# Opening of a hybrid decoder layer: half of the squares and of the modulation rows moved to VectorE, copies and factor work reordered

## The chip, the cores and the metric

The kernel runs on one core of one Trainium2 chip. The metric is the device time of one execution in microseconds (us); shorter is better. A core has TensorE (PE, matmuls), VectorE (DVE), ScalarE (ACT), GpSimd (POOL) and SyncE (SP, which issues most DMAs). Each engine works through its own queue of instructions in order and waits on semaphores for results of the others.

## What is computed

One layer, float32, for 1024 tokens of 2048 features:

```python
mod = silu(c) @ w_ada + b_ada              # c: (1, 2048), w_ada: (2048, 6144)
shift, scale, gate = split(mod, 3)
h = rms_norm(x, gain) * (1 + scale) + shift   # x: (1024, 2048)
proj = h @ w_in                            # (1024, 8192): q, k, v, z of two groups of 8 heads
oa = stick_breaking_attention(...) * silu(z_sb)
ob = group_norm(retention(...)) * silu(z_r)
out = x + gate * (concat(oa, ob) @ w_out)
```

The change lies in what comes ahead of `proj` and in its first part: the row norms of x, `mod`, h and its first products.

## The kernel before, in words

**Products in three passes.** A float32 product is made of three fast ones (`mm3`, L184 to L187): each operand is cut into a high part, which ScalarE writes (L172 for weights, L595 for h), and a low part, which VectorE writes as a difference (L174, L597). `wp` holds four high and four low tiles of weights, so that a block's weights can be cut two blocks ahead and no more.

**The opening.** 16 blocks of 128 features (`kc`) are walked in the order `KCS`, by the index p. Tokens come in two halves of 512 (hf 0 and 1).

1. `load_x` brings x of tokens 0 to 511 as 16 tiles of 128 tokens by 512 features. `x_squares` (L510) lets ScalarE square each tile and sum its rows; `x_scale` (L519) works out 1/rms with 13 small VectorE instructions on a column and scales the tiles, half on VectorE, half on ScalarE.
2. w_ada is read in chunks `cc` of 256 columns, 2 MB each (`load_ada`): chunks 0 to 7 give the scale, chunks 8 to 15 the shift. `ada_sums` (L559) adds up a chunk's 16 rows of each partition with 16 products on PE (each is two passes of the array, 32 instructions of 32x256 in all), into a bank `accp` that VectorE copies out (L569). `ada_mod` (L576) adds over the partitions with two small products `mod`, and VectorE turns them into `mods` (L585, L586) or `shift` (L588).
3. `x_turn` (L538) turns four 128x128 pieces of x on PE into a bank, and copies the bank to `xT`, by VectorE for odd p of the first half (L550), else by ScalarE (L552). `make_h` (L590) writes h's two parts from `xT` and `mods`.
4. `start_mm` multiplies h of block p by 7 heads of weights ("first": z of the retention group), 21 matmuls to a block. In the first half's loop over p, sums of chunk p//2+2 come at the start of each odd block, and `ada_mod` of the chunk after p's within each even block, behind head 4.

**The second half** (tokens 512 to 1023) does the same with the 16 blocks again. In block p, in PE's order: head 0; `x_turn` of block p+2; heads 1 to 3; then `ada_mod` (even p, whose result is `shift`) or `ada_sums` (odd p); heads 4 to 6. `x_turn`, `ada_sums` and `ada_mod` share one bank, "C", so each waits until the last one's result has been read. `cut_w` cuts the weights of block p+2 at the end of block p, and `add_bias` (L769) multiplies the raw weights by the shift on VectorE.

**Factors.** The rest of `proj` is done as a Strassen-like product, which wants sums and differences of quarters of h. `factors(ks)` (L622) queues them for two k at a time: eight ScalarE instructions `whole` (L629: scale and shift of `xT`; they read `shift`) and B21's parts go to the deque `urgent`, 28 more (differences on VectorE, L635 and L642; high parts on ScalarE, L605; low parts on VectorE, L612, with stores for T2, T1 and B22) go to `background`. Behind each head of the second half, `some` takes one or two from each deque. `factors` is called at the end of blocks 3, 7, 11 and 15; what is left after block 15 runs in the first groups of the next stage.

**The next stage** begins with products `pj` into four banks in which the heads 3 to 6 of "first" have been gathered; ScalarE must have copied them out first (`spill`, zt, L775), behind the cuts of the stage's first weights.

**Order.** PE's order is the order of the program text (`manual_schedule`). On VectorE and ScalarE a scheduler orders the first half's instructions by its own estimates; from the second half on every engine takes the order of the text.

**The end.** `finish_out` (L1475) multiplies the output's last bank by the gate, adds x, and stores 128x512 through SP.

Of the kernel before, what the change touches and what calls it, by code (L numbers as in the profile page):

```python
# [98 lines left out]
def layer_kernel(ctx, tc, x, c, w_ada, b_ada, norm_gain, w_in, sb_q_gain, sb_k_gain, ret_norm_gain, w_out,  # L99
# [410 lines left out]
    def x_squares(ts):  # L510
        ss = sm.tile([P, 2, 4], F32, tag="ss", name=f"ss_{ts[0]}")
        for i, t in enumerate(ts):
            for qt in range(4):
                junk = get(f"junk_{t}_{qt}")
                nc.scalar.activation(junk, xt[t, qt], AF.Square, accum_out=ss[:, i, qt:qt + 1])
                put(junk)
        return ss

    def x_scale(ts, ss):  # L519

        n = len(ts)
        nc.vector.tensor_tensor(ss[:, 0:n, 0:2], ss[:, 0:n, 0:2], ss[:, 0:n, 2:4], op=ALU.add)
        m = sm.tile([P, 2], F32, tag="m", name=f"m_{ts[0]}")
        nc.vector.tensor_tensor(m[:, 0:n], ss[:, 0:n, 0], ss[:, 0:n, 1], op=ALU.add)
        nc.vector.tensor_scalar(m[:, 0:n], m[:, 0:n], 1.0 / D, EPS, op0=ALU.mult, op1=ALU.add)
        y = sm.tile([P, 2], F32, tag="y", name=f"y_{ts[0]}")
        u = sm.tile([P, 2], F32, tag="u", name=f"u_{ts[0]}")
        rsqrt_newton(y[:, 0:n], m[:, 0:n], u[:, 0:n])
        for qt in (0, 2, 1, 3):
            for i, t in enumerate(ts):  # L530
                if i % 2:
                    nc.scalar.activation(xt[t, qt], xt[t, qt], AF.Copy, scale=y[:, i:i + 1])
                else:
                    nc.vector.tensor_scalar(xt[t, qt], xt[t, qt], y[:, i:i + 1], None, op0=ALU.mult)
# [3 lines left out]
    def x_turn(p, g, tag, bufs):  # L538

        kc = KCS[p]  # L540
        xT[kc, g] = get(f"xT{kc}_{g}")
        tp = ps.tile([P, HALF], F32, tag=tag, bufs=bufs, name=f"xtp_{kc}_{g}")
        for t in range(4):
            src = xt[4 * g + t, kc // 4]
            nc.tensor.transpose(tp[:, t * P:(t + 1) * P], src[:, (kc % 4) * P:(kc % 4 + 1) * P], ident)
        left_in[kc // 4, g] -= 1
        if left_in[kc // 4, g] == 0:
            put(*[xt.pop((4 * g + t, kc // 4)) for t in range(4)])
        if p % 2 and g == 0:
            nc.vector.tensor_copy(xT[kc, g], tp)  # L550
        else:
            nc.scalar.activation(xT[kc, g], tp, AF.Copy)  # L552
# [6 lines left out]
    def ada_sums(cc):  # L559
# [3 lines left out]
        for j in range(16):  # L563
            g = j % 4
            nc.tensor.matmul(ap_[32 * g:32 * g + 32, :], silu_z[:, j, :],  # L565
                             ada[cc, j // 2][:, (j % 2) * 256:(j % 2) * 256 + 256], start=j < 4, stop=j >= 12)
        put(*[ada.pop((cc, g)) for g in range(8)])
        acc = get(f"acc_{cc}")
        nc.vector.tensor_copy(acc[:, 0:256], ap_)  # L569
# [129 lines left out]
    sums = {0: ada_sums(0)}  # L699
    for p in range(4):  # L700
        x_turn(p, 0, "pj", 4)
# [3 lines left out]
    for p in range(2):  # L705
        make_h(p, 0)
    for p in range(4, 8):
# [3 lines left out]
    sums[1] = ada_sums(1)  # L711
# [13 lines left out]
    sums[2] = ada_sums(2)  # L725
# [3 lines left out]
    for p in range(2, KC):  # L729
# [7 lines left out]
        if p % 2 and p < KC - 1:  # L737
            sums[cc + 1] = ada_sums(cc + 1)
# [43 lines left out]
    for p in range(KC):  # L782
# [11 lines left out]
        for i, h in enumerate((0, 1, 2, 3, 4, 5, 6) if p < KC - 1 else (3, 4, 5, 6, 0, 1, 2)):  # L794
# [3 lines left out]
            if i == 3 and p % 2 == 0:  # L798
                ada_mod(cc, sums.pop(cc))
            if i == 3 and p % 2 and cc < 15:  # L800
# [3 lines left out]
            if len(urgent) <= 6:  # L804
                some(background, 1 if urgent or i % 4 == 3 else 2)
            some(urgent, 1 if p < KC - 1 else 2)
# [4 lines left out]
        if p % 4 == 3:  # L811
            factors((KCS[p - 3], KCS[p - 2]))
# [662 lines left out]
    def finish_out(n, t, bank_):  # L1475
        x_, y_ = xrs.pop((n, t)), anywhere(f"yt_{n}_{t}")
        nc.vector.tensor_tensor(y_, bank_, gates[n], op=ALU.mult)
# [108 lines left out]
```

## Time and profile before

| | us |
|---|---|
| median of 3 runs | 1971.6 (1971.21 to 1973.71) |
| the profiled execution's own time | 1972.75 |
| its span, first to last instruction | 1971.0 |
| PE busy | 1918.2 (97% of the span) |
| VectorE busy | 1222.5 (62%) |
| ScalarE busy | 800.0 (41%) |
| granted PE clock, mean | 0.995 |

The profiled execution's own time is 1.75 us above its span. A row of a timeline gives the start, the duration, the engine, the source line, the operation and its tiles; in brackets stand the idle time of the engine just before and what ended it. A row of a wait table gives who waited for whom, the sum, the number and the longest. A row of a windows table gives, for each engine, the busy time in that stretch and the number of instructions, then the granted PE clock, the share of the DMA engines and GB/s.

### The profile page before, as it was taken

How to read it: one execution, taken by the hardware profiler on the slowest of the kernel's cores; microseconds unless marked ns; L12 is line 12 of the kernel's file. 1: busy time of each engine (PE TensorE's matmuls, PEld its weight loads, DVE VectorE, ACT ScalarE, POOL GpSimd, SP SyncE). 2: the span in 40 equal slices, each digit the busy share in tenths (PEclk: the TensorE clock that was granted, in tenths of full speed). 3: DMA queues.
4: the chain of work that ended last, by engine and by line, in shares of the span. 5: the costliest groups of instructions: out<-in, count | busy, mean ns of one | idle time of the engine just before them, and what ended most of it. 6: DMA issues, size and time to landing. Idle time of an engine off the chain costs nothing.

```text
span 1971.0 us, 28290 instructions
## 1 busy us (share of the span) xinstructions
PE 1918.2 (97%) x9703; PEld 1573.3 (80%) x9703; DVE 1222.5 (62%) x2389; ACT 800.0 (41%) x1497; POOL 81.1 (4%) x278
## 2 busy tenths in 40 slices
PE   5999899999999999999999999999999999999998
PEld 4776678787888878888888888887888888788887
DVE  4637875346768676867686767865677557634222
ACT  5446663224544454445444544343343554211110
POOL 0000000000110011001100010000000000000000
PEclk9999989999999999999999999999999999999999
DMA  9967797897797679867976798889979738546141
GB/s 321 355 216 262 254 335 268 287 339 261 243 305 262 239 238 302 272 234 241 305 269 240 244 299 270 258 270 295 317 236 284 229 107 282 194 123 198 38 138 64
DMA packets 381724, 487.50 MB, mean 247 GB/s; under 512 B 30734, under 2 KB 201864, under 8 KB 381580
## 3 DMA queue, kind: packets, MB, share of 16 engines
q1 hardware_dynamic: 381192, 485.65, 75.3%
q8 instruction: 76, 1.25, 0.3%
q14 instruction: 68, 0.56, 0.1%
q10 hardware_dynamic: 388, 0.04, 0.0%
HBM read 410.04 MB, written 75.54 MB: 246 GB/s over the span
## 4 chain that ended last, share of the span: by engine, by line
PE 85%; DVE 6%; DMA 5%; ACT 2%; issue 1%; SPq 0%; DVEq 0%; ACTq 0%
PE pj L185 17%; PE pj L187 17%; PE pj L186 16%; PE y L185 5%; PE y L187 5%; PE y L186 5%; PE first L185 2%; PE first L186 2%; PE first L187 2%; PE accp L565 2%; DVE wl L174 1%; PE tp_B L1070 1%; PE zp L185 1%; PE zp L187 1%; PE zp L186 1%
## 5 line engine op out<-in xcount | busy, mean ns | idle before, releaser
L174 DVE TENSOR_TENSOR wl<-A,wh 128x512 fp32r<-128x512 f32 x392 | 272.6, 696 | 315.1 <-ACT wh L172 295.4
L172 ACT ACTIVATE wh<-A 128x512 fp32r<-128x512 f32 x392 | 246.4, 629 | 359.0 <-PE pj L186 340.6
L185 PE MATMUL y<-wh_o,ch 128*128 128x512 f32 x512 | 200.1, 391 | 2.4 <-ACT ch L1412 2.3
L187 PE MATMUL y<-wh_o,cl 128*128 128x512 f32 x512 | 199.6, 390 | 0.0
L186 PE MATMUL y<-wl_o,ch 128*128 128x512 f32 x512 | 199.3, 389 | 0.0
L174 DVE TENSOR_TENSOR wl_o<-wo,wh_o 128x512 fp32r<-128x512 f32 x80 | 54.9, 691 | 173.9 <-ACT wh_o L172 169.9
L172 ACT ACTIVATE wh_o<-wo 128x512 fp32r<-128x512 f32 x80 | 50.4, 630 | 238.4 <-PE y L187 214.2
L388 ACT ACTIVATE c<-pj 128x512 f32<-128x512 f32 x112 | 66.5, 597 | 173.3 <-PE pj L187 148.1
L391 DVE TENSOR_TENSOR c<-pj,c 128x512 f32<-128x512 f32 x112 | 75.0, 688 | 79.2 <-PE pj L187 79.2
L185 PEld LDWEIGHTS y<-wh_o,ch 128*128 128x128 f32 x512 | 96.1, 188 | 24.4 <-ACT ch L1412 3.1
L187 PEld LDWEIGHTS y<-wh_o,cl 128*128 128x128 f32 x512 | 96.1, 188 | 21.1 <-DVE cl L1413 1.1
L186 PEld LDWEIGHTS y<-wl_o,ch 128*128 128x128 f32 x512 | 96.1, 188 | 19.9
L295 DVE TENSOR_TENSOR A<-A,A 128x512 f32<-128x512 f32 x160 | 109.4, 691 | 2.1
L185 PE MATMUL pj<-B21h,wh 128*128 128x512 f32 x232 | 94.5, 407 | 4.4 <-ACT zt L775 4.4
L1050 DVE TENSOR_TENSOR_SCAN om<-om 128x128 f32<-128x128 f32 (+2 forms) x96 | 93.6, 974 | 1.1
L185 PE MATMUL first<-h_hi,wh_first 128*128 128x512 f32 x224 | 92.6, 413 | 1.1 <-ACT h_hi L595 1.1
L187 PE MATMUL pj<-B21h,wl 128*128 128x512 f32 x232 | 92.7, 399 | 0.7 <-DVE wl L174 0.7
L185 PE MATMUL pj<-T1h,wh 128*128 128x512 f32 x232 | 92.5, 399 | 0.0
L185 PE MATMUL pj<-B22h,wh 128*128 128x512 f32 x232 | 92.3, 398 | 0.0
L186 PE MATMUL pj<-B21l,wh 128*128 128x512 f32 x232 | 92.1, 397 | 0.0
L185 PE MATMUL pj<-B11h,wh 128*128 128x512 f32 x232 | 91.7, 395 | 0.0
L187 PE MATMUL pj<-T1h,wl 128*128 128x512 f32 x232 | 90.7, 391 | 0.0
(237 smaller groups left out, 4580.5 us busy)
## 6 DMA issues: line engine op xcount, KB each, us to landing
A<-in_w_in_dram SPq DMA_DIRECT2D x228, 256.0 KB
ada<-in_w_ada_dram SPq DMA_DIRECT2D x128, 256.0 KB
wo<-in_w_out_dram SPq DMA_DIRECT2D x80, 256.0 KB
gr<-in_w_ada_dram SPq DMA_DIRECT2D x64, 256.0 KB
T2h<-fac_T SPq DMA_DIRECT2D x56, 256.0 KB
T2l<-fac_T SPq DMA_DIRECT2D x56, 256.0 KB
T1h<-fac_T SPq DMA_DIRECT2D x56, 256.0 KB
T1l<-fac_T SPq DMA_DIRECT2D x56, 256.0 KB
```

What stands on the lines that cost most here:

```text
L172: nc.scalar.activation(hi[:, 0:n], src[:, 0:n], AF.Copy)
L174: nc.vector.tensor_tensor(lo[:, 0:n], src[:, 0:n], hi[:, 0:n].bitcast(F32), op=ALU.subtract)
L185: nc.tensor.matmul(o, a_hi, b_hi, start=first, stop=False, skip_group_check=on)
L186: nc.tensor.matmul(o, a_hi, b_lo, start=False, stop=False, skip_group_check=on)
L187: nc.tensor.matmul(o, a_lo, b_hi, start=False, stop=last, skip_group_check=on)
L295: nc.vector.tensor_tensor(r[o], r[a], r[b], op=ALU.add if n == 1 else ALU.subtract)
L388: nc.scalar.activation(t, o, AF.Copy)
L391: nc.vector.tensor_tensor(dst[q, cc], o, dst[q, cc], op=ALU.add)
L565: nc.tensor.matmul(ap_[32 * g:32 * g + 32, :], silu_z[:, j, :], ada[cc, j // 2][:, (j % 2) * 256:(j % 2) * 256 + 256], start=j < 4, stop=j ...
L1050: nc.vector.tensor_tensor_scan(rev, rev, rev, init, op0=ALU.mult, op1=ALU.bypass)
L1070: nc.tensor.transpose(banks_[j // 2][:, c0:c0 + P], be[:, j * P:(j + 1) * P], ident)
```

## The change

- `x_squares`: ScalarE squares two of a token tile's four quarters; for the other two VectorE takes `bn_stats`, and `bn_aggr` over both gives mean and variance. `x_scale` puts the two together (two small VectorE instructions more per call, and `bn_aggr`).
- `ada_sums` has a parameter: for chunks 1 to 7 PE sums 8 of the 16 rows, and VectorE adds the other 8, one `scalar_tensor_tensor` of 128x256 each, the first of them from the bank. The copy of the bank falls away there.
- Opening: the turns of blocks 0 and 1 stand ahead of chunk 0's last four products; the copies of blocks 2 and 3 come, in the program text, behind `make_h` of blocks 0 and 1.
- Second half: `ada_mod` and `ada_sums` come behind head 4 in place of head 3. `factors` is called behind `ada_mod` in blocks 2, 6, 10 and 14 (for the same two k), in place of the end of blocks 3, 7, 11 and 15. `some` takes 2 from `background` behind even heads and 1 behind odd ones (or 1 while `urgent` holds something), and 1 from `urgent` in the last block too.
- The last output tile is finished and stored in two halves, by SP and by ScalarE's DMA queue.

```diff
@@ -508,21 +508,28 @@
                               ada_rows[:, 2 * g:2 * g + 2, col:col + 2 * P])
 
     def x_squares(ts):
-        ss = sm.tile([P, 2, 4], F32, tag="ss", name=f"ss_{ts[0]}")
+
+        ss = sm.tile([P, 2, 2], F32, tag="ss", name=f"ss_{ts[0]}")
+        mv = sm.tile([P, 2, 2], F32, tag="xmv", name=f"xmv_{ts[0]}")
         for i, t in enumerate(ts):
-            for qt in range(4):
-                junk = get(f"junk_{t}_{qt}")
-                nc.scalar.activation(junk, xt[t, qt], AF.Square, accum_out=ss[:, i, qt:qt + 1])
+            st6 = sm.tile([P, 2, 6], F32, tag="xst6", name=f"xst6_{t}")
+            for j in range(2):
+                junk = get(f"junk_{t}_{j}")
+                nc.scalar.activation(junk, xt[t, j], AF.Square, accum_out=ss[:, i, j:j + 1])
                 put(junk)
-        return ss
-
-    def x_scale(ts, ss):
-
-        n = len(ts)
-        nc.vector.tensor_tensor(ss[:, 0:n, 0:2], ss[:, 0:n, 0:2], ss[:, 0:n, 2:4], op=ALU.add)
+                nc.vector.bn_stats(st6[:, j, :], xt[t, 2 + j])
+            nc.vector.bn_aggr(mv[:, i, :], st6)
+        return ss, mv
+
+    def x_scale(ts, sums):
+
+        n, (ss, mv) = len(ts), sums
         m = sm.tile([P, 2], F32, tag="m", name=f"m_{ts[0]}")
         nc.vector.tensor_tensor(m[:, 0:n], ss[:, 0:n, 0], ss[:, 0:n, 1], op=ALU.add)
         nc.vector.tensor_scalar(m[:, 0:n], m[:, 0:n], 1.0 / D, EPS, op0=ALU.mult, op1=ALU.add)
+        nc.vector.tensor_tensor(mv[:, 0:n, 0], mv[:, 0:n, 0], mv[:, 0:n, 0], op=ALU.mult)
+        nc.vector.tensor_tensor(mv[:, 0:n, 0], mv[:, 0:n, 0], mv[:, 0:n, 1], op=ALU.add)
+        nc.vector.scalar_tensor_tensor(m[:, 0:n], mv[:, 0:n, 0], 0.5, m[:, 0:n], op0=ALU.mult, op1=ALU.add)
         y = sm.tile([P, 2], F32, tag="y", name=f"y_{ts[0]}")
         u = sm.tile([P, 2], F32, tag="u", name=f"u_{ts[0]}")
         rsqrt_newton(y[:, 0:n], m[:, 0:n], u[:, 0:n])
@@ -535,7 +542,7 @@
 
     left_in = {(qt, g): 4 for qt in range(4) for g in range(2)}
 
-    def x_turn(p, g, tag, bufs):
+    def x_turn(p, g, tag, bufs, now=True):
 
         kc = KCS[p]
         xT[kc, g] = get(f"xT{kc}_{g}")
@@ -546,27 +553,42 @@
         left_in[kc // 4, g] -= 1
         if left_in[kc // 4, g] == 0:
             put(*[xt.pop((4 * g + t, kc // 4)) for t in range(4)])
-        if p % 2 and g == 0:
-            nc.vector.tensor_copy(xT[kc, g], tp)
-        else:
-            nc.scalar.activation(xT[kc, g], tp, AF.Copy)
+
+        def copy():
+            if p % 2 and g == 0:
+                nc.vector.tensor_copy(xT[kc, g], tp)
+            else:
+                nc.scalar.activation(xT[kc, g], tp, AF.Copy)
+        if now:
+            copy()
+        return copy
 
     silu_t = get("silu_z")
     silu_z = silu_t.rearrange("p (j n) -> p j n", n=32)
     nc.vector.memset(silu_t, 0.0)
     nc.vector.tensor_copy(silu_z[:, :, 0], silu_c)
 
-    def ada_sums(cc):
+    def ada_sums(cc, n_pe=16, between=None):
+
 
 
         ap_ = ps.tile([P, 256], F32, tag="C", name=f"accp_{cc}")
-        for j in range(16):
+
+        def row(j):
+            return ada[cc, j // 2][:, (j % 2) * 256:(j % 2) * 256 + 256]
+
+        for j in range(n_pe):
+            if between and j == n_pe - 4:
+                between()
             g = j % 4
-            nc.tensor.matmul(ap_[32 * g:32 * g + 32, :], silu_z[:, j, :],
-                             ada[cc, j // 2][:, (j % 2) * 256:(j % 2) * 256 + 256], start=j < 4, stop=j >= 12)
+            nc.tensor.matmul(ap_[32 * g:32 * g + 32, :], silu_z[:, j, :], row(j), start=j < 4, stop=j >= n_pe - 4)
+        acc = get(f"acc_{cc}")
+        if n_pe == 16:
+            nc.vector.tensor_copy(acc[:, 0:256], ap_)
+        for j in range(n_pe, 16):
+            nc.vector.scalar_tensor_tensor(acc[:, 0:256], row(j), silu_c[:, j:j + 1],
+                                           ap_ if j == n_pe else acc[:, 0:256], op0=ALU.mult, op1=ALU.add)
         put(*[ada.pop((cc, g)) for g in range(8)])
-        acc = get(f"acc_{cc}")
-        nc.vector.tensor_copy(acc[:, 0:256], ap_)
         return acc
 
     mods = cons.tile([P, KC], F32, name="mods")
@@ -696,19 +718,20 @@
     ss = [x_squares((0, 1)), x_squares((2, 3))]
     x_scale((0, 1), ss[0])
     x_scale((2, 3), ss[1])
-    sums = {0: ada_sums(0)}
-    for p in range(4):
-        x_turn(p, 0, "pj", 4)
+    sums = {0: ada_sums(0, between=lambda: [x_turn(p, 0, "pj", 4) for p in range(2)])}
+    copies = [x_turn(p, 0, "pj", 4, False) for p in range(2, 4)]
     ws[0] = start_w(0, 0)
     load_ada(1)
     ada_mod(0, sums.pop(0))
     for p in range(2):
         make_h(p, 0)
+    for copy in copies:
+        copy()
     for p in range(4, 8):
         x_turn(p, 0, "pj", 4)
     start_mm(0, 0, ws[0], range(3))
     ws[1] = start_w(1, 0)
-    sums[1] = ada_sums(1)
+    sums[1] = ada_sums(1, 8)
     load_ada(2)
     for p in range(8, 12):
         x_turn(p, 0, "pj", 4)
@@ -722,7 +745,7 @@
     start_mm(1, 0, ws.pop(1), range(3, NZ))
     for p in range(2):
         put(h_hi.pop((KCS[p], 0)), h_lo.pop((KCS[p], 0)))
-    sums[2] = ada_sums(2)
+    sums[2] = ada_sums(2, 8)
     load_ada(3)
     ws[3] = start_w(3, 0)
     rawz = {}
@@ -735,7 +758,7 @@
         for t in X_LOAD.get(p, ()):
             load_x(t)
         if p % 2 and p < KC - 1:
-            sums[cc + 1] = ada_sums(cc + 1)
+            sums[cc + 1] = ada_sums(cc + 1, 8 if cc < 7 else 16)
             load_ada(cc + 2)
         if p in X_STAT:
             x_scale(X_STAT[p], x_squares(X_STAT[p]))
@@ -795,21 +818,21 @@
             start_mm(p, 1, w, (h,))
             if i == 0 and p + 2 < KC:
                 x_turn(p + 2, 1, "C", 1)
-            if i == 3 and p % 2 == 0:
+            if i == 4 and p % 2 == 0:
                 ada_mod(cc, sums.pop(cc))
-            if i == 3 and p % 2 and cc < 15:
+                if p % 4 == 2:
+                    factors((KCS[p - 2], KCS[p - 1]))
+            if i == 4 and p % 2 and cc < 15:
                 sums[cc + 1] = ada_sums(cc + 1)
             if i == 2 and p + 2 < KC:
                 make_h(p + 2, 1)
             if len(urgent) <= 6:
-                some(background, 1 if urgent or i % 4 == 3 else 2)
-            some(urgent, 1 if p < KC - 1 else 2)
+                some(background, 1 if urgent or i % 2 else 2)
+            some(urgent, 1)
         put(h_hi.pop((KCS[p], 1)), h_lo.pop((KCS[p], 1)))
         if p + 2 < KC:
             ws[p + 2] = cut_w(p + 2, 1, rawz[p + 2])
         add_bias(p)
-        if p % 4 == 3:
-            factors((KCS[p - 3], KCS[p - 2]))
     put(silu_t)
     background.extendleft(reversed(urgent))
     background.extend(late)
@@ -1474,6 +1497,14 @@
 
     def finish_out(n, t, bank_):
         x_, y_ = xrs.pop((n, t)), anywhere(f"yt_{n}_{t}")
+        if (n, t) == (3, 7):
+            for i, eng in enumerate((nc.sync, nc.scalar)):
+                sl = slice(i * 2 * P, (i + 1) * 2 * P)
+                nc.vector.tensor_tensor(y_[:, sl], bank_[:, sl], gates[n][:, sl], op=ALU.mult)
+                nc.vector.tensor_tensor(y_[:, sl], y_[:, sl], x_[:, sl], op=ALU.add)
+                eng.dma_start(out[0][t * P:(t + 1) * P, n * HALF + i * 2 * P:n * HALF + (i + 1) * 2 * P], y_[:, sl])
+            put(x_, y_)
+            return
         nc.vector.tensor_tensor(y_, bank_, gates[n], op=ALU.mult)
         nc.vector.tensor_tensor(y_, y_, x_, op=ALU.add)
         put(x_)
```

## The prediction

> **What bounds the kernel now.** I read the page first, then busy times by stretch, then PE's waits up to 340 us.
>
> ```profile
> PE 1918.2 (97%) x9703; PEld 1573.3 (80%) x9703; DVE 1222.5 (62%) x2389; ACT 800.0 (41%) x1497; POOL 81.1 (4%) x278
> ```
> ```profile
> 24.71:118.70 93.99, 92.60 (x638) 70.58 (x637) 54.19 (x147) 41.42 (x86) 0.00 (x0) 1.00 0.97 326
> 118.70:160.00 41.30, 41.30 (x247) 32.51 (x246) 18.03 (x32) 19.80 (x35) 0.00 (x0) 1.00 0.76 254
> 160.00:244.00 84.00, 75.90 (x465) 56.42 (x463) 67.75 (x117) 54.34 (x95) 0.00 (x0) 0.98 0.75 247
> 244.00:256.40 12.40, 7.34 (x16) 5.29 (x17) 8.64 (x15) 12.32 (x23) 0.00 (x0) 0.59 0.82 297
> ```
> ```profile
> PE accp L565 <- DMA ada<-in_w_ada_dram: 8.7, 1, 8.7
> PE accp L565 <- ACT xT L552: 5.0, 2, 2.5
> PE pj L185 <- ACT zt L775: 4.4, 1, 4.4
> PE xtp L545 <- DVE shift L588: 2.4, 2, 1.2
> ...
> PE pj L187 <- DVE wl L174: 0.7, 1, 0.7
> ```
>
> PE is the bound: 97% busy. The change acts ahead of 260 us, apart from the last store. From 24.7 to 160 us PE hardly waits, so only fewer PE instructions or an earlier start can shorten that part. From 160 to 244 us PE is idle for 8.1 us, mostly behind a copy of `xT` or `shift`, and for 5.1 more (4.4 and 0.7) where the next stage begins. VectorE is 58% busy in the first stretch and 81% in the third: what the change gives it lands on an engine with little left.
>
> **The opening: -0.85.**
>
> ```profile
> 18.95 5.83 PE L565 MATMUL accp<-ada,silu_z 128*32 128x256 f32 x32 [8.74 <-DMA ada<-in_w_ada_dram]
> ...
> 29.92 0.49 PE L185 MATMUL first<-h_hi,wh_first 128*128 128x512 f32 x1 [1.09 <-ACT h_hi L595]
> 30.70 0.50 PE L186 MATMUL first<-h_lo,wh_first 128*128 128x512 f32 x1 [0.29 <-DVE h_lo L597]
> ...
> 34.61 1.97 PE L545 MATMUL xtp<-ident,x 128*128 128x128 f32 x16
> ```
>
> Chunk 0's products are paced by its landing, so quicker squares of x bring nothing by themselves; x need only be scaled before the turns of blocks 0 and 1. Those eight turns (half of the row of 1.97 for sixteen) move into the wait. But in the built order of the changed kernel ScalarE still has the copies of blocks 2, 4 and 6, and VectorE those of 3, 5 and 7, ahead of h's parts; only blocks 0 and 1 come off the way. I put the second product at 29.85 in place of 30.70. Ends: 0, and -2.4 (1.0 of turns, waits of 1.09 and 0.29).
>
> **PE's rows: -6.5.**
>
> ```profile
> 53.69 1.86 PE accp L565 x32
> 65.83 1.86 PE accp L565 x32
> ...
> 102.25 1.86 PE accp L565 x32
> ```
>
> Half a chunk's products take 0.93 us; seven chunks, 6.5. The period between two chunks falls from 12.14 to 11.2.
>
> **VectorE in the first half: +3.5 of new PE waits.**
>
> ```profile
> 451.55 0.48 DVE L861 SCALAR_TENSOR_TENSOR ga<-gr,silu_c,ga 128x256 f32<-128x256 f32 x1
> 451.95 0.69 DVE L295 TENSOR_TENSOR A<-A,A 128x512 f32<-128x512 f32 x1
> ```
> ```profile
> 1713.75 2.04 DVE L861 SCALAR_TENSOR_TENSOR ga<-gr,silu_c,ga 128x256 f32<-128x256 f32 x4
> ```
> ```profile
> 1608.10 0.89 DVE L1281 BATCH_NORM_STATS2 st<-op 128x6 f32<-128x128 f32 x4
> ```
> ```profile
> L174 DVE TENSOR_TENSOR wl_first<-wr,wh_first 128x512 fp32r<-128x512 f32 x17 | 11.7, 691 | 14.9 <-ACT wh_first L172 14.9
> ...
> L174 DVE TENSOR_TENSOR wl_first<-wr,wh_first 128x384 fp32r<-128x384 f32 x17 | 9.4, 554 | 3.0 <-ACT wh_first L172 3.0
> ...
> L569 DVE COPY acc<-accp 128x256 f32<-128x256 f32 x9 | 3.8, 423 | 5.2 <-PE accp L565 5.2
> L164 DVE SCALAR_TENSOR_TENSOR u<-u,m 128x1 f32<-128x1 f32 x12 | 1.9, 160 | 0.4
> ```
>
> The gate's sums use the instruction of the new rows: 0.52 us each behind one another ((2.04 - 0.48) / 3), 0.40 with something else between. Eight cost 3.2 to 4.1; the copy, 0.42, goes. The first reads the bank, a form that no row shows: ends 0.4 and 0.6, taken as the others.
>
> `bn_stats` is shown with 128 elements, 0.2 us apart. Another VectorE row grows by 0.137 us from 384 to 512 elements; three such steps give 0.6 for 512 (ends 0.2 and 0.8). Two of them, the aggregate, and two small instructions of 0.2 make 1.8 us for each of the token tiles 4 to 7, whose squares fall into blocks 4 to 11. For each of those four periods VectorE had some 8.4 us of work (two weight cuts 2.2, two h parts 1.3, thirteen small 2.5, four scalings 1.7, copy and mods 0.7) and now has 13 to 14, against 11.2 of PE. It works in order, so the excess falls on what stands behind: a chunk's sum, for which `mod` waits, and weights' low parts. Followed through the built order, PE waits 0.75 for chunk 2's sum (eight rows in a run, 4.2 us, against 3.5 of products), 0.3 for chunk 4's, and 1 and 1.5 for the weights of blocks 10 and 12, which stand behind seven rows and x's small instructions. Sum 3.5; 0 if the small ones fit between rows, 6.5 if each period is 0.8 longer.
>
> ```profile
> 12.22 6.23 SPq L507 DMA_DIRECT2D ada<-in_w_ada_dram  x8
> ...
> 82.74 4.87 SPq L507 DMA_DIRECT2D ada<-in_w_ada_dram  x8
> ```
>
> Loads cost nothing: chunk 0's products end 6.3 us after its last issue (18.45, 24.78), chunk 7 is issued by 87.6 and used at 102.25, so 8 us are spare, and PE comes 5 earlier at most. The rows hold tiles of w_ada a few us longer, inside the same reserve. ScalarE's saved squares were off the path.
>
> The first half so ends **3.9 us** sooner (0.85 + 6.5 - 3.5).
>
> **The second half's loop: +1.1.**
>
> ```profile
> 145.33 0.60 PE L545 MATMUL xtp<-ident,x 128*128 128x128 f32 x4
> ```
> ```profile
> 243.56 0.39 PE L187 MATMUL first<-h_hi,wl_first 128*128 128x512 f32 x1
> ```
>
> Block 2's turn to the end of block 15 takes 98.6 us. Factor work now begins 1.5 blocks earlier and comes as some 11 tasks a block, where it was 1, 9, 13 and 5: good for bank C. Against it: `whole` stands right behind the `shift` that it reads, on ScalarE, with the next weights' high parts behind it, and VectorE's low parts wait for those. VectorE's 67.75 us from 160 to 244 (11 1/2 blocks) are 24 per four blocks; PE needs 26. So VectorE's idle time becomes PE's: `shift` and the copy of `accp` stand behind factor work, and the next turn waits for them. In the built order I get PE waits of 1.8, 1.8, 1.0, 0.9, 2.3 us in blocks 5 to 9, and the like up to 13: 99.7 us. Ends: -8.1 (all idle time of today's loop gone) and +5.
>
> **The boundary: +2.4.**
>
> ```profile
> 236.48 0.50 PE L580 MATMUL mod<-ones,acc 128*128 128x1 f32 x4
> ```
> ```profile
> 241.24 0.15 DVE L588 TENSOR_TENSOR shift<-mod,cols 128x2 f32<-128x2 f32 x1
> ```
> ```profile
> 246.17 1.65 ACT L172 ACTIVATE wh<-A 128x512 fp32r<-128x512 f32 x3
> 247.73 3.49 ACT L775 ACTIVATE zt<-first 128x512 f32<-128x512 f32 x7
> ...
> 251.59 2.95 ACT L629 ACTIVATE xT<-xT,shift,mods 128x512 f32<-128x512 f32 x4
> ```
>
> Today the last block's eight `whole` run behind zt, where PE waits for nothing; queued in block 14 they stand ahead of it. The last `shift` comes 4.3 us after its `mod`, and in the new order too. Behind it ScalarE does eight `whole` (0.72 apart: 5.7), two high parts (1.1), 0.65 of waiting for a difference, three cuts (1.65), the first zt (0.5): 9.6 us. PE's last product of the loop ends 2.1 us after `shift`, so PE waits 7.5 in place of 5.1. Ends: 3.5 (-1.6) if `shift` comes at once, 9 (+3.9).
>
> **The clock: 0.**
>
> ```profile
> 184.32 3.33 PE L565 MATMUL accp<-ada,silu_z 128*32 128x256 f32 x32 [2.50 <-ACT xT L552]
> ```
> ```profile
> 216.64 1.93 PE L565 MATMUL accp<-ada,silu_z 128*32 128x256 f32 x32 [2.53 <-ACT xT L552]
> ```
>
> After one wait of 2.50 us PE ran at half speed (3.33 for 1.93), after one of 2.53 not. With five or six waits of about 2 us in the new loop I keep one such spell (ends -1.4 and +3.6), and the half-speed stretch behind the boundary (0.59 in the fourth stretch) as it is. [...]
>
> **The tail: -0.3.**
>
> ```profile
> 1965.66 0.69 DVE L1478 TENSOR_TENSOR yt<-yt,xr 128x512 f32<-128x512 f32 x1 [0.91 <-DMA xr<-in_x_dram]
> ...
> 1966.98 0.69 DVE L1478 TENSOR_TENSOR yt<-yt,xr 128x512 f32<-128x512 f32 x1
> ```
>
> The last add waits in line behind an x tile that lands late. Halving it lets half of the store leave some 0.5 us earlier; two more instruction starts take 0.2 back. Ends 0 and -0.7.
>
> **Sum.** -3.9 + 1.1 + 2.4 + 0 - 0.3 = -0.7, against the profiled execution's own 1972.75: 1972.0. That execution is 1.15 above the median 1971.6, so on the runs' scale I predict **1971.0**. 0.2% (3.9 us) is about what a measurement of this kernel can tell from no change.
>
> **Rivals.**
>
> *VectorE keeps pace.* If the small instructions vanish between rows and `shift` is not late, the first half gains 7.4, loop and boundary stay: -7.7, 1963.9. For: only 58% busy today. Against: 13 us of work in 11.2. 0.25. If also the loop's idle 8.1 us go, 1956: 0.05.
>
> *The boundary and the loop cost more than the rows save.* `whole` behind a late `shift` and ahead of zt: the boundary costs +3.9, the loop +3, one more half-speed spell 1.8, the first half gains 2.8 only: +5.9, 1977.5. It decides from the point where `shift` lags `mod` by over 5 us. For: VectorE at 81%, and today's 4.3. Against: the earlier start. 0.27.
>
> *The copies are not overtaken*: counted already, since the built order shows it.
>
> **Chances.** Forecast 0.43; VectorE keeps pace 0.25 and 0.05; slower rival 0.27. Faster by over 0.2% 0.30, within 0.43, slower 0.27. The range 1963 to 1978 takes in forecast, first and slower rival and leaves out the 1956 case and the outer ends of terms. The likeliest case alone: 1968 to 1975.
>
> **What would show it.** Right: second product near 29.9; accp rows of 16 instructions and 0.93; PE waits for `acc` or `wl` between 45 and 110 us, about 3.5; chunk 8's sums near 110.5 in place of 114.4; waits on `shift` and `acc` in blocks 5 to 13; a wait on zt of over 6 us. Wrong: no wait on VectorE in the first half, zt waited for less than 5 us, or loop waits under 6 us.

## The result, and the profile after

| | before | after |
|---|---|---|
| median | 1971.57 us (12 runs, 1967.99 to 1973.71) | 1977.17 us (12 runs, 1974.14 to 1979.21) |
| the profiled execution's own time | 1972.75 | 1979.21 |
| its span | 1971.0 | 1977.2 |

After over before is 1.0028, 95% interval 1.0019 to 1.0037: 0.28% or 5.6 us **slower**. The forecast was no change (1971.0), so the direction was wrong, though the time lies inside the range, near its upper end and next to the slower rival's 1977.5.

The busy line of the page: PE lost 112 matmuls and 3.8 us of work, VectorE gained 28 us.

```profile
PE 1914.4 (97%) x9591; PEld 1568.4 (79%) x9591; DVE 1250.6 (63%) x2476; ACT 789.4 (40%) x1465; POOL 81.1 (4%) x278
```

**The opening**, PE's timeline after (start, duration; the idle time ahead in brackets). Before, chunk 0's products ended at 24.78, the second product came at 30.70 and chunk 1's sums at 32.75.

```profile
24.46 1.39 PE L552 MATMUL xtp<-ident,x 128*128 128x128 f32 x8
25.78 0.64 PE L584 MATMUL accp<-ada,silu_z 128*32 128x256 f32 x8
...
27.28 0.50 PE L602 MATMUL mod<-ones,acc 128*128 128x1 f32 x4
...
30.95 0.49 PE L185 MATMUL first<-h_hi,wh_first 128*128 128x512 f32 x1 [1.37 <-ACT h_hi L617]
31.74 0.64 PE L186 MATMUL first<-h_lo,wh_first 128*128 128x512 f32 x1 [0.29 <-DVE h_lo L619]
...
35.30 1.07 PE L584 MATMUL accp<-ada,silu_z 128*32 128x256 f32 x16
```

In this execution the second product is 1.04 later, not 0.85 earlier. Of this, 0.87 is the chunk's landing: PE took up its sixth tile at 23.46, before at 22.59. The eight turns stand where PE waited for the last two tiles, but they took 1.39 (the next eight took 1.09), and chunk 0's last products end at 26.42. From the second product to chunk 1's sums it takes 3.56 us in place of 2.05: the products have the length of half speed (0.64 where 0.39 is usual), and the granted clock is 0.50 from 31.94 to 35.35.

What VectorE did meanwhile:

```profile
22.45 1.68 DVE L541 TENSOR_SCALAR x<-x,y 128x512 f32<-128x512 f32 x4
...
28.19 1.16 DVE L174 TENSOR_TENSOR wl_first<-wr,wh_first 128x512 fp32r<-128x512 f32 x2
29.27 0.15 DVE L607 TENSOR_TENSOR mods<-mod,scale_b 128x2 f32<-128x2 f32 x1
```

VectorE scales x until 24.1 (23.6 before). This does not hold up the turns: blocks 0 and 1 need only the first quarter of each token tile, which VectorE and ScalarE scale first, here by 23.2. `mods`, whose `mod` was done at 27.8, stands behind both low parts of block 0's weights, as it did before.

**The first half's rows** came out as forecast. VectorE's groups from 30 to 118 us by form (line, shapes, number; busy time and mean ns; idle time before):

```profile
L589 DVE SCALAR_TENSOR_TENSOR acc<-ada,silu_c,acc 128x256 f32<-128x256 f32 x49 | 23.6, 481 | 0.5
...
L520 DVE BATCH_NORM_STATS2 xst<-x 128x6 f32<-128x512 f32 x8 | 5.3, 685 | 0.0
...
L589 DVE SCALAR_TENSOR_TENSOR acc<-ada,silu_c,accp 128x256 f32<-128x256 f32 x7 | 3.4, 480 | 5.1 <-PE accp L584 5.1
```

A row costs 0.48 us from the bank too, `bn_stats` over 512 elements 0.69 (taken: 0.6). Chunk 8's sums:

```profile
113.73 1.93 PE L584 MATMUL accp<-ada,silu_z 128*32 128x256 f32 x32
```

From chunk 1's sums to chunk 8's that is 78.4 us, before 81.6 (32.75 to 114.32): -3.1, forecast -3.0. With the late start, 0.6 of it is left at this point.

**The loop and the boundary**, PE's waits from 24.71 to 300 us (total, times, longest):

```profile
PE pj L185 <- ACT zt L798: 7.3, 1, 7.3
PE xtp L552 <- DVE shift L610: 5.9, 5, 2.0
PE xtp L552 <- DVE acc L587: 4.6, 3, 1.6
PE mod L602 <- ACT xT L561: 1.6, 2, 1.1
PE first L185 <- ACT h_hi L617: 1.4, 1, 1.4
PE first L187 <- DVE wl_first L174: 1.3, 1, 1.3
PE pj L185 <- ACT wh L172: 1.2, 1, 1.2
PE mod L602 <- DVE acc L589: 0.7, 1, 0.7
PE accp L584 <- ACT xT L561: 0.6, 2, 0.3
```

From the turn in block 2 (called block 2's turn) to the end of block 15, busy times after:

```profile
144.78:247.84 103.06, 90.41 (x560) 66.61 (x558) 80.12 (x139) 64.95 (x114) 0.00 (x0) 1.00 0.79 263
```

PE has the same work as before (98.62 with 90.57 busy); its idle time in the loop has gone from 8.1 to 12.7. At the boundary it waits 7.3 for zt (before 4.4, and 0.7 for weights). The account of the two profiled executions:

| stretch | before | after | difference | forecast |
|---|---|---|---|---|
| to the second product | 30.70 | 31.74 | +1.0 | -0.85 |
| to chunk 1's sums | 2.05 | 3.56 | +1.5 | 0 |
| to chunk 8's sums | 81.57 | 78.43 | -3.1 | -3.0 |
| block 2's turn to the end of block 15 | 98.62 | 103.06 | +4.4 | +1.1 |
| boundary (zt, then wl) | 5.1 | 7.3 | +2.2 | +2.4 |
| PE's last product to the end | 5.83 | 5.69 | -0.1 | -0.3 |

### The profile page after: what moved, and what is told of

Same layout as the page of the kernel before. It is cut to its first block, busy times and chain, and to the rows that moved or that the text cites. A ratio compares the mean times of both kernels' runs of the same rounds, so it can differ in the third digit from the quotient of the medians.

```text
span 1977.2 us, 28111 instructions
## 1 busy us (share of the span) xinstructions
PE 1914.4 (97%) x9591; PEld 1568.4 (79%) x9591; DVE 1250.6 (63%) x2476; ACT 789.4 (40%) x1465; POOL 81.1 (4%) x278
## 4 chain that ended last, share of the span: by engine, by line
PE 79%; DMA 8%; DVE 8%; ACT 3%; issue 2%; SPq 1%; ACTq 0%; DVEq 0%
PE pj L185 16%; PE pj L186 16%; PE pj L187 16%; PE y L185 5%; PE y L186 5%; PE y L187 5%; PE first L185 2%; PE first L187 1%; PE first L186 1%; DVE wl L174 1%; PE accp L584 1%; PE zp L185 1%; PE tp_B L1093 1%; PE zp L187 1%; PE zp L186 1%
## 5 line engine op out<-in xcount | busy, mean ns | idle before, releaser
L185 PE MATMUL y<-wh_o,ch 128*128 128x512 f32 x512 | 200.7, 392 | 2.4 <-ACT ch L1435 2.3
L187 PE MATMUL pj<-B22h,wl 128*128 128x512 f32 x232 | 90.7, 391 | 0.0
```

Source lines behind the costliest of these rows:

```text
L185: nc.tensor.matmul(o, a_hi, b_hi, start=first, stop=False, skip_group_check=on)
L187: nc.tensor.matmul(o, a_lo, b_hi, start=False, stop=last, skip_group_check=on)
```

## The experiments

Two theories stood at first: **A**, the new order of the second half is the loss; **B**, VectorE's extra work of the first half runs on. "Ratio" is always to the kernel before on the same chip, with its 95% interval. The runs come from four chips, so two kernels are compared by their ratios; the medians alone can be off by 1 to 2 us (the kernel before: 1971.20 to 1972.94).

| kernel | median us | ratio | interval |
|---|---|---|---|
| old loop | 1969.28 | 0.9991 | 0.9982 to 1.0001 |
| new loop alone | 1981.10 | 1.0050 | 1.0037 to 1.0064 |
| all squares on ScalarE | 1977.88 | 1.0037 | 1.0024 to 1.0050 |
| old opening | 1977.22 | 1.0028 | 1.0018 to 1.0038 |
| head 3 | 1976.94 | 1.0028 | 1.0018 to 1.0038 |
| third and fourth round late | 1970.45 | 0.9995 | 0.9986 to 1.0003 |
| squares and rows | 1967.01 | 0.9975 | 0.9966 to 0.9985 |
| rows | 1967.28 | 0.9976 | 0.9965 to 0.9987 |
| second round late too | 1973.61 | 1.0001 | 0.9992 to 1.0009 |
| fourth round late | 1966.75 | 0.9963 | 0.9950 to 0.9976 |
| new opening alone | 1972.40 | 0.9996 | 0.9985 to 1.0006 |
| old opening, fourth round late | 1965.80 | 0.9969 | 0.9958 to 0.9979 |
| new loop alone, fourth round late | 1969.97 | 0.9995 | 0.9985 to 1.0005 |

### The second half, out and in

Old loop: the changed kernel with the second half's order put back, the counts of tasks too.

```diff
-            if i == 4 and p % 2 == 0:
+            if i == 3 and p % 2 == 0:
                 ada_mod(cc, sums.pop(cc))
-                if p % 4 == 2:
-                    factors((KCS[p - 2], KCS[p - 1]))
...
         add_bias(p)
+        if p % 4 == 3:
+            factors((KCS[p - 3], KCS[p - 2]))
```

> The changed kernel with the second half's order put back (sums and mods behind head 3, factors at the end of blocks 3, 7, 11 and 15, the old counts of tasks); the opening, the rows on VectorE and the end stay changed. Theory A, the new order of the second half is the loss (in the profile of the changed kernel 103.1 us from block 2's turn to the end of block 15 in place of 98.6, and 7.3 in place of 5.1 at the boundary): block 2's turn stays near 144.8, the loop takes 98.6, zt is waited for 4 to 5 us, the next stage starts near 248, and the time falls by 6 to 7 to about 1970.8. Rival B, VectorE's extra work of the first half runs on into the second and delays the loop whatever its order: the loop still takes over 101, time 1974 or more.

Measured: 1969.28, so 7.9 below the changed kernel (7.3 by the ratios). The loop from chunk 8's sums (113.21) to the end of block 15 (241.18) takes 128.0; after, 134.1 (113.73 to 247.84). Its waits, from 130 to 250 us:

```profile
PE accp L584 <- ACT xT L561: 5.0, 2, 2.5
PE pj L185 <- ACT zt L798: 4.4, 1, 4.4
PE xtp L552 <- DVE shift L610: 2.3, 2, 1.2
```

They are those of the kernel before, though the first half's VectorE work is that of the change. A holds, B falls.

New loop alone: the kernel before with that hunk alone, in the other direction.

> The kernel before with the second half's new order alone. Theory A: block 2's turn at 145.3 as before, loop 103, a wait of 7.3 on zt, next stage at about 255.5; 6 to 7 slower than the kernel before, about 1978. Rival B: the loop is no more than 1 longer without the first half's extra VectorE work, boundary +2.2; at most 1974.5.

Measured: 1981.10, 9.9 slower than before, even more than expected; waits of 7.3 on zt, 5.3 and 3.8 for shift and acc, and 2.0 on the next stage's weights.

### The opening

All squares on ScalarE: `x_squares` and `x_scale` of the changed kernel as before.

> The changed kernel with all squares of x on ScalarE again. In the changed kernel the second product starts at 31.74 and at half speed, chunk 1's sums at 35.30 (before: 30.70 and 32.75). Theory O1, the longer VectorE chain of x makes the opening late (x scaled 0.54 later): the second product comes at 30.8 or earlier, chunk 1's sums by 33.3, and as 1.8 us of VectorE work also leaves each of blocks 4 to 11, the wait of 1.33 for block 12's weights goes: 3 to 4 faster than the changed kernel, about 1973.5. Rival O2, the turns of blocks 0 and 1 ahead of chunk 0's last products make it late: chunk 0's last products still end past 26, the second product comes past 31.3; 1.5 faster at most, about 1976.

Old opening: no `between`, the copies of blocks 2 and 3 at once.

```diff
-    sums = {0: ada_sums(0, between=lambda: [x_turn(p, 0, "pj", 4) for p in range(2)])}
-    copies = [x_turn(p, 0, "pj", 4, False) for p in range(2, 4)]
+    sums = {0: ada_sums(0)}
+    for p in range(4):
+        x_turn(p, 0, "pj", 4)
```

> The changed kernel with the old order of the opening (chunk 0's sums unbroken, turns of blocks 0 to 3 behind them with their copies at once); squares stay halved. O1: x is still 0.54 later than before, so the second product comes at about 31.2, time within 1 of the changed kernel, 1976.5. O2: chunk 0's sums end at 24.8 as before, mod comes at 26.5, the second product at 30.7 to 30.9 at full speed, chunk 1's sums near 33: 1.5 to 2.5 faster, about 1975.

Measured: 1977.88 and 1977.22. Neither gives anything that the times can tell, so both expectations of a gain (O1's in the first run, O2's in the second) missed: the opening is not where the 5.6 us lie. One reason lies in the profiles: the start itself moves from one execution to the next. With the old order of the opening chunk 0's products end between 24.66 and 25.93 in eight executions of different kernels, the second product always 5.92 later; with the new order they end between 24.65 and 26.76 in seven, the second product 5.32 later. A late start in one profile is not the change's.

What the order itself does is seen from the moment when PE takes up the chunk's sixth tile, which stands ahead of the turns in both orders. With the old order the second product starts 8.02 to 8.11 later in all eight executions. With the new one it starts 7.54, 7.54 and 7.63 later in three (fourth round late; third and fourth round late; head 3), and 8.07, 8.28, 8.52 and 8.60 later in the other four. The means are 8.05 and 8.03. In the three the turns do fill the wait, as was forecast; fourth round late:

```profile
23.22 1.09 PE L552 MATMUL xtp<-ident,x 128*128 128x128 f32 x8
24.24 0.64 PE L584 MATMUL accp<-ada,silu_z 128*32 128x256 f32 x8
```

In the three the eight turns take 1.09, as the next eight do; in the four they take 1.18, 1.39, 1.63 and 1.71. In the changed kernel (1.39) the first three matmuls take 0.48, 0.42 and 0.36 us, the other five 0.27 each. So what the order saves is lost again where the turns take longer.

New opening alone: the kernel before with the new opening order and the halved last store.

> The kernel before with the new opening order (turns of blocks 0 and 1 ahead of chunk 0's last four rows, copies of blocks 2 and 3 behind h's parts in the text) and the halved last store alone. Theory O3, nothing is gained since x is scaled only when the chunk's last tile lands, the turns then stand ahead of the chunk's last products, and VectorE still does both first low parts of weights ahead of mods: the second product comes 6.6 to 7.0 after PE took the chunk's last tile up or could have (6.6 in the kernel before); time within 0.7 of the kernel before. Rival C, it costs 2 or more, as the two runs with the old second half, with and without it, differ (1969.3 and 1967.0): half-speed products behind the second one. The forecast's own term, -0.85, would give 1970.7 and a second product at 5.8.

Measured: 0.9996 of before, no change: C falls. The interval (3.0 faster to 1.2 slower) holds both O3 and the forecast's -0.85, and O3's reason, x scaled too late, is not what the traces show. Its opening in PE's timeline:

```profile
31.30 0.50 PE L185 MATMUL first<-h_hi,wh_first 128*128 128x512 f32 x1 [1.37 <-ACT h_hi L610]
32.08 0.50 PE L186 MATMUL first<-h_lo,wh_first 128*128 128x512 f32 x1 [0.28 <-DVE h_lo L612]
32.42 0.44 PE L187 MATMUL first<-h_hi,wl_first 128*128 128x512 f32 x1
32.66 0.63 PE L185 MATMUL first<-h_hi,wh_first 128*128 128x512 f32 x1
```

From the last line to 34.79 the products stand 0.43 apart, where 0.23 is usual: half speed again, in mid-run. This spell, 1.2 to 1.5 us, came in three of the seven executions with the new order (wait of 1.37 ahead of the first product) and in none of the eight with the old (1.1); the three are those in which the eight turns took longest. Three pairs of kernels differ in the opening alone. The old one takes the ratio from 0.9991 (old loop) to 0.9975 (squares and rows), leaves it at 1.0028 (changed kernel, old opening), and takes it from 0.9963 to 0.9969 (fourth round late). What the new opening costs among the other parts, if anything, so stays open.

### Where the loop's loss comes from

Head 3: the changed kernel with sums and mods behind head 3 again.

> The changed kernel with the second half's sums and mods behind head 3 again; factors are called right behind the mods as in the change. In the changed kernel PE waits 5.9 (5 times) for shift and 4.6 (3 times) for acc before a turn, 1.6 and 0.6 for a copy of xT. Theory H, bank C: one head later leaves VectorE one head (three products, 0.7) less before the next turn wants the bank; so the eight waits shrink by about 0.7 each, 10.5 to about 5, those for xT grow to 3 to 5, and the loop from block 2's turn takes 98 to 100; time about 1973.5. Rival Q, factor work queued on VectorE ahead of shift and acc: the eight waits together stay over 8, loop 102 or more, time within 2 of the changed kernel. Boundary in both 7.3.

Measured: 1976.94, nothing gained, where H asked for 1973.5. Waits from 130 to 250 us:

```profile
PE xtp L552 <- DVE shift L610: 4.1, 3, 1.4
PE mod L602 <- ACT xT L561: 4.1, 5, 1.6
PE accp L584 <- ACT xT L561: 3.9, 3, 1.7
PE xtp L552 <- DVE acc L587: 1.3, 2, 0.7
```

The waits for shift and acc shrink as theory H says (10.5 to 5.4), and those for xT grow from 2.2 to 8.0: 13.4 in place of 12.7. The head chosen only says at which of the bank's three users PE waits.

Third and fourth round late: in the changed kernel, `factors` early in blocks 2 and 6 only.

```diff
-                if p % 4 == 2:
+                if p % 4 == 2 and p < 10:
                     factors((KCS[p - 2], KCS[p - 1]))
...
+        if p % 4 == 3 and p > 8:
+            factors((KCS[p - 3], KCS[p - 2]))
```

> The changed kernel with only the first two rounds of factors called early (blocks 2 and 6); the third and fourth are called at the end of blocks 11 and 15 as before; head 4 and the counts of tasks stay. Theory R, each round of factors costs PE some 4 us of waits while turns and sums of the loop still depend on VectorE and ScalarE, and the earlier calls put a third round ahead of the last turns (in the kernel before the third round falls behind them, no wait from 217 on): the loop's waits fall from 12.6 to about 8, the wait on zt from 7.3 to 4.5, and 6 to 7 are gained: about 1970.5. Rival Q, the new places of the sums and the counts cost by themselves: waits of 2 us remain in blocks 12 and 13, the loop stays over 101, only the boundary's 2 to 3 come back: about 1974.5.

Measured: 1970.45, the time that R asked for: the loop's waits fall from 12.7 to 9.5, that on zt to 5.3, and the 1.2 for weights behind it is gone, 6.4 together. Which of the two late rounds brings it is open here.

Fourth round late: in the changed kernel, only block 14's call goes back to the end of block 15.

```diff
-                if p % 4 == 2:
+                if p % 4 == 2 and p < 14:
                     factors((KCS[p - 2], KCS[p - 1]))
...
+        if p == 15:
+            factors((KCS[p - 3], KCS[p - 2]))
```

> The changed kernel with only the last round of factors (block 14's) called at the end of block 15 as before. Theory W, the last round's eight whole on ScalarE ahead of zt make the boundary longer: the wait on zt falls from 7.3 to 4.4 to 5.3, the loop stays at 103 within 1, and 2 to 3 are gained: about 1974.7. Rival T, the third round's work is what stands ahead of zt: the wait stays over 6.5, time within 1 of the changed kernel.

Measured: 1966.75, ratio 0.9963: **faster than both kernels**, and some 8 us more than W asked for. The loop is as expected no better (133.6 from chunk 8's sums at 110.72 to the end of block 15 at 244.34), but the wait on zt is gone altogether. ScalarE across the boundary, first the changed kernel, then this one:

```profile
245.50 2.93 ACT L651 ACTIVATE xT<-xT,shift,mods 128x512 f32<-128x512 f32 x4 [2.75 <-DVE shift L610]
248.33 0.61 ACT L627 ACTIVATE B21h<-xT 128x512 fp32r<-128x512 f32 x1
248.85 0.80 ACT L651 ACTIVATE xT<-xT,shift,mods 128x512 f32<-128x512 f32 x1
...
250.84 2.21 ACT L651 ACTIVATE xT<-xT,shift,mods 128x512 f32<-128x512 f32 x3
252.96 1.65 ACT L172 ACTIVATE wh<-A 128x512 fp32r<-128x512 f32 x3
254.52 3.48 ACT L798 ACTIVATE zt<-first 128x512 f32<-128x512 f32 x7
```
```profile
239.14 1.14 ACT L172 ACTIVATE wh<-A 128x512 fp32r<-128x512 f32 x2
242.11 0.63 ACT L172 ACTIVATE wh<-A 128x512 fp32r<-128x512 f32 x1 [1.84 <-PE first L186]
242.65 3.51 ACT L798 ACTIVATE zt<-first 128x512 f32<-128x512 f32 x7
```

In the changed kernel ScalarE stands idle for 2.75 us at a `whole` that waits for the last shift, does eight of them, and only then cuts the next stage's weights and empties the banks. Without that call it has cut the weights before the loop ends and copies each bank as it is finished. PE's first products of the next stage, the same two kernels:

```profile
255.14 0.80 PE L185 MATMUL pj<-B21h,wh 128*128 128x512 f32 x1 [7.30 <-ACT zt L798]
```
```profile
244.18 0.39 PE L185 MATMUL pj<-B21h,wh 128*128 128x512 f32 x1
244.41 0.39 PE L186 MATMUL pj<-B21l,wh 128*128 128x512 f32 x1
```

After the wait PE also runs its next 12 products at half speed (granted clock 0.50 up to 260.63; 0.43 apart in place of 0.23: 2.4 us), and at 293.4 meets a second wait of 1.2 on weights. All this together, from chunk 8's sums to the first products `nm` further on:

```profile
L947 PE MATMUL nm<-qs,ones x64: 379/391/403, 451.6 to 1107.6; 128*32 128x256 f32 x64
```
```profile
L949 PE MATMUL nm<-qs,ones x64: 379/391/403, 438.1 to 1093.5; 128*32 128x256 f32 x64
```

337.9 us after (113.73 to 451.6) and 327.4 without the last call (110.72 to 438.1): 10.5 us for one call in these two profiles, 0.65% or some 13 us by the ratios. Single profiles scatter: the same stretch takes 326.6 to 331.2 in the five kernels with the old loop and no round moved.

This also corrects R. With the third round late as well, the loop is 3.0 shorter (130.7 from chunk 8's sums to the end of block 15), but the wait of 5.3 on zt is there, and the ratio is 0.9995 in place of 0.9963. The gain of the run with both rounds late came from the fourth alone; calling the third late costs some 6 us on balance. R's time was met by luck.

New loop alone, fourth round late: the same edit in the kernel before with the new loop alone.

> The kernel before with the new order of the second half alone, but the last round of factors at the end of block 15. With that round at block 14 too, this order alone was 9.9 slower (1981.1). Theory W, the last round's call is what makes the new order a loss: the loop takes 134 to 135 from chunk 8's sums (129.6 before) and the wait on zt goes from 5.1 to nothing; within 2 of the kernel before, if anything faster. Rival L, the order of the loop is a loss of its own without the first half's gain: 3 or more slower than the kernel before, with a wait on zt of over 3.

Measured: 0.9995 of before, where the new loop with that call had 1.0050. W holds, free of the first half's parts: there is no wait on zt, the new order of the loop costs about what the boundary then gives back, and the last call is the loss. Only the loop is longer than W said, 136.1 in place of 134 to 135; two spells of half speed lie in it (products 0.43 apart from 199.0 to 200.7 and from 233.1 to 234.8). From chunk 8's sums to `nm` it is 327.9, against 339.3 in the new loop with that call.

### The parts that gain

Squares and rows: the changed kernel with the old opening and the old loop.

> The changed kernel with the old opening order and the old second half: halved squares, eight rows of seven chunks on VectorE, and the halved last store are left. Theory A: the first half as in the run with the old opening order (79.2 from the second product to chunk 8's sums, where the kernel before has 83.6), the loop and the boundary as in the run with the old loop: 4 to 5 faster than the kernel before, about 1967. Rival B, the gain of the first half is lost again in waits of the second: 1970 or more.

Rows: the kernel before with the rows and the halved last store alone.

> The kernel before with eight rows of seven chunks on VectorE and the halved last store alone; all squares on ScalarE. Theory V, VectorE's load decides the first half: with 1.8 us less for each of four tiles no wait for acc or weights is left over 0.5, chunk 8's sums come 80 or less after the second product minus 1, 78.5; 0.5 to 1 faster than the run with halved squares too, about 1966. Rival S, the scheduler's order decides: as in the run of the changed kernel with all squares on ScalarE, block 12's weights are waited for by 1.8, 81 from the second product to chunk 8's sums; about 1968.5.

Measured: 1967.01 and 1967.28, both faster than before by about 0.25%: A of the first run holds, and its B falls. From the second product to chunk 8's sums it is 79.2 and 78.5, as A and V said, and from chunk 1's sums 77.2 and 76.5. But V's 0.5 to 1 us of gain is not in the times, and the wait of 0.7 for chunk 2's sum is left in both: whether the squares stay on ScalarE makes no difference that the times can tell. No run with rows and the old opening has the wait for block 12's weights, nor has the new opening without the rows. All six kernels with the rows and the new opening have it, 1.3, or 1.8 with all squares on ScalarE. It so needs the order that the scheduler makes of the new opening together with the rows; taking the squares off VectorE does not remove it.

Second round late too: squares and rows, with the second round of factors called at the end of block 11.

```diff
-        if p % 4 == 3:
-            factors((KCS[p - 3], KCS[p - 2]))
+        for q in {3: (3,), 11: (7, 11), 15: (15,)}.get(p, ()):
+            factors((KCS[q - 3], KCS[q - 2]))
```

> The run with halved squares and rows and the old second half (1967.0), with the second round of factors called at the end of block 11, together with the third, in place of the end of block 7. Theory R, a round costs PE some 4 us of waits only while turns and sums still depend on VectorE and ScalarE: the second pair of waits (0.33, 1.19 and 2.50 between 200 and 212) goes, the loop is 4 shorter, the boundary stays at 4.4 and 0.7, and what is left over of the factors fits into the next stage, where VectorE is half idle: about 1963. Rival B, the left-over work is late there: PE waits for factors or weights in the first groups of the next stage, or the wait on zt grows past 7, and the time is 1967 or more.

Measured: 1973.61, ratio 1.0001 where the run without it has 0.9975, some 5 us slower: B. The second pair of waits did go from the loop, but the work turns up in the next stage. Waits from 24 to 420 us:

```profile
PE pj L185 <- ACT T3h L627: 8.0, 2, 5.2
PE pj L185 <- ACT zt L797: 3.4, 1, 3.4
...
PE pj L186 <- DVE T3l L634: 1.7, 1, 1.7
```

So here too R is only half of it: a round left for later is free only as far as the next stage doesn't need its factors at once.

Old opening, fourth round late: the changed kernel with both edits.

> The changed kernel with the old opening order and with only the last round of factors back at the end of block 15: halved squares, rows, the new loop with rounds at blocks 2, 6 and 10, and the halved last store. Theory A, the parts add: from the second product to chunk 8's sums 79.2 (80.5 in the run with only the last round moved back), the loop at 133.5 to 134.3 from chunk 8's sums to the end of block 15, no wait on zt: 1 to 2 faster than that run, some 8 faster than the kernel before, about 1964.5 where that has 1972. Rival B, the parts do not add: as the run with only the last round moved back, or slower, 1966 or more.

Measured: 0.9969 of before, within the interval of the run with only the fourth round late (0.9963). A asked for 0.9962, which lies in this run's interval too, so the times cannot tell A from B. In the profiles it gains 1.3 us up to chunk 8's sums (79.3 from the second product, against 80.5) and is 1.9 longer from there to the end of block 15 (135.5 against 133.6), though PE waits 1.3 less in that loop. Two spells of half speed account for it: PE's granted clock is 0.50 from 193.9 to 197.3 and from 228.0 to 231.4, and 1.00 throughout the loop of the other.

## Why the prediction was wrong

**PE's rows and VectorE's new waits: right in size.** Net -3.1 measured, -3.0 forecast; the wait for chunk 2's sum 0.7 (0.75), for block 12's weights 1.3 (1.5). Those for block 10's weights, put at 1, and for chunk 4's sum, put at 0.3, are not in the table, so the waits that are named make 2.0 of the 3.5, and the agreement of the sum is in part luck. The one of 1.3 also goes with the new opening and not with VectorE's load alone. With the old opening 4 to 5 us were to be had here.

**The opening: wrong.** The step "those eight turns move into the wait" is right in three of seven executions, and then saves 0.4 to 0.5 in place of 0.85. What it left out is the speed of PE in that wait: in the other four the turns took 1.18 to 1.71 in place of 1.09, and on average nothing is saved. The +2.5 of the one profile is 0.87 of later landing, slow turns, and 1.5 of a later spell of half speed.

**The loop: this is the step that failed. Right in its mechanism, too small in its sum.** PE waits for shift and acc where it was said, 10.5 us of the 12.7. The forecast's 99.7 leaves 9.1 of idle time over the 90.6 of work, and 7.8 of it was followed out for blocks 5 to 9 (measured there: 5.9). So only 1.3 was left for "the like up to 13", where four more blocks like these would have given some 6: measured are 6.8 in blocks 10 to 13, three of them (1.63, 1.09 and 1.96 from 221 to 231) from the third round, which before fell behind the last turns. The term came out at +4.4 in place of +1.1, above the +3 of the slower rival, and 6.1 against the old loop's profile without a half-speed spell (134.1 and 128.0).

**The boundary: right in size, +2.2 of +2.4, and in its mechanism**: shift 4.3 behind its mod, eight `whole`, the cuts, then zt. What the forecast missed is what it could have been: it compared 7.5 with today's 5.1, while the same loop without the last call has no wait on zt at all. The call's price is 10.5 in the profiles, not 2.4. The slower rival had the time (1977.5) and in part the way: it put the loop at +3 and one more half-speed spell at 1.8 (1.5, but in the opening). Its condition, shift lagging by over 5, did not come: shift lagged by 4.3, and the boundary cost 2.2 in place of its 3.9.

**The clock: 0 by luck.** The forecast kept one spell of half speed in the loop. The changed kernel's profile has none there (granted clock 1.00 from 144.78 to 247.84) and one in the opening. **The tail: -0.1** from PE's last product to the end, with -0.3 forecast; too small to matter.

**VectorE keeps pace**, the faster rival at 0.25, came nearest in the runs with the old opening and the old loop: 4 to 5 us faster than before in place of its 7.7. It needed the loop left alone.

## What to carry to other kernels

When work is queued earlier on an engine that works in order, ask what stands behind it at the next boundary: here one call put eight instructions that wait for a late value ahead of the copies that free the banks, and cost 10.5 us, while the same call in three earlier places cost nothing on balance. Move such calls one at a time. Work that is moved into a wait of PE is done at the speed that PE has there: the same eight turns took 1.09 us in some executions and up to 1.71 in others, which ate what the move saved. Before counting on a term below 1 us, look at how much the start moves between executions (here 1.3 us and more).

## What was not expected of the hardware

After waits of 2.50 to 2.53 us PE ran at half speed in some executions and not in others. The same line in two runs, rows and then squares and rows:

```profile
179.87 3.52 PE L577 MATMUL accp<-ada,silu_z 128*32 128x256 f32 x32 [2.50 <-ACT xT L554]
```
```profile
180.99 1.93 PE L584 MATMUL accp<-ada,silu_z 128*32 128x256 f32 x32 [2.52 <-ACT xT L561]
```

Over six kernels whose loop has such waits this happened after 3 of 11 of them, and after 1.37 us at the opening in 3 of 7. Such a spell costs 1.2 to 1.6 us, as much as several of the terms that were forecast.

Busy times around these two waits (PE's stands first, the granted clock behind POOL's), the same two runs:

```profile
176.31:179.72 3.41, 1.06 (x5) 0.53 (x3) 2.33 (x5) 2.47 (x6) 0.00 (x0) 1.00 0.63 203
179.72:183.13 3.41, 3.26 (x32) 1.38 (x32) 3.41 (x7) 2.27 (x5) 0.00 (x0) 0.50 0.18 65
```
```profile
176.37:179.78 3.41, 2.10 (x10) 1.38 (x8) 2.63 (x4) 1.40 (x3) 0.00 (x0) 1.00 0.83 261
179.78:183.20 3.42, 2.21 (x34) 1.24 (x35) 3.12 (x6) 3.33 (x7) 0.00 (x0) 1.00 0.21 77
```

In the first run PE is busy for 1.06 us from 176.31 to 179.72, and the granted clock is 0.50 from 179.72 to 183.13. In the second it is busy for 2.10 us from 176.37 to 179.78 and for 2.21 from there to 183.20, and the granted clock is 1.00 in both stretches. The length of the wait does not tell the two apart: in the run of the new opening alone the same line took 1.93 after both of its waits, 2.50 us each. What does is not settled by these runs.
